# A planner that counts ScalarE's function tables, fewer filling products, and a split burst, in a two-layer recurrent trunk

## The chip, the cores and the metric

The kernel runs on one core of one Trainium2 chip. The metric is device time in microseconds (us) for one launch, the median of several executions. PE is the matrix engine (TensorE), DVE is VectorE, ACT is ScalarE, POOL is GpSimd and SP is the engine that issues most DMAs.

## The reference

One step of a two-layer decoder trunk over 1024 prompt tokens and 32 sample tokens (8 sequences of 4), width 1024, in fp32. Layer 1 is an RG-LRU block, layer 2 an HGRN2 block.

```python
def _rmsnorm(x, gain):
    return x * lax.rsqrt(jnp.mean(x * x, axis=-1, keepdims=True) + EPS) * gain

def _lru_layer(...):                          # layer 1
    u = _rmsnorm(x) @ w_in                    # 1024 x 3072
    xb, gate = u[..., :W_LRU], u[..., W_LRU:]
    xc = causal_conv(xb)                      # 4 taps
    r, ig = sigmoid(xc @ w_r + b_r), sigmoid(xc @ w_i + b_i)   # 16 blocks of 96
    a = exp(-8 * softplus(-lam) * r)
    h = scan(a, sqrt(1 - a * a) * ig * xc)
    return x + (h * silu(gate)) @ w_out       # 1536 x 1024

def _hgrn_layer(...):                         # layer 2, 8 heads of 128
    q, f, v, gate = split(_rmsnorm(x) @ w_in) # 1024 x 4096
    g = lb + (1 - lb) * sigmoid(f); k = 1 - g
    o, S = chunked_linear_recurrence(silu(q), k, v, log(g))
    return x + (norm(o) * silu(gate)) @ w_out # then a final rmsnorm
```

## The kernel before, in words

All 1056 tokens lie along the free axis, in three chunks of 352 (in layer 2's second half in quarters of 264). Every fp32 weight and activation is split into a high and a low part, and `mm3` (lines 246 to 251) makes one product of 128 input rows as three matmuls, high by high, high by low, low by high. A product over 1024 input rows is eight such steps into one of the `mm` banks of PSUM; the next product into a bank waits until the earlier one has been read. In the `hg` banks lie all smaller products: the norms' sums and their spread over the partitions, the LRU gates, the attention of layer 2.

**The order is written by a planner.** Each operation is recorded in a `Flow` with its engine, a cost in us, what it reads and writes, and a priority. `plan` runs a list schedule over these costs, `back` turns it into due times, `run` repeats this eight times and `search` tries 3000 random changes of the due times in the first 60 us; then the operations are emitted, engine by engine, in the planned order. Products of the main chain (`main=True`) keep the order in which they were recorded; everything else is placed by the planner. The hardware follows that order on each engine, whatever the times turn out to be. Layer 1 with the first products of layer 2 is one `Flow`, the rest a second.

**The start.** The weights and the first chunk come in by DMA. ACT makes the high parts (L390 for weights, L872 for activations), DVE the low parts (L333, L878), ACT the squares (L442), DVE adds them (L445). The first chunk's six products (three of the gates, three of the convolution; their weights lie in `whi`, `X`, `yh` and `yl`) use activations that are not yet normalised. `norm` follows for each of the three chunks: PE sums the squares over the partitions (L286), ACT takes three square roots (L457), DVE inverts them (L459) and lays them on diagonals (L460, L463), and PE spreads them by a product with ones (L465). The first chunk's products are scaled by this when they are read (L539, L492), the other chunks' activations before they are used (L470, L333). Filling products of ones by ones (L740), `WARM` of them, have the lowest priority: the planner places one where PE would otherwise have nothing.

**Function tables.** ACT computes Sqrt from one table and Tanh, Exp and Silu from another; plain copies, squares and scalings need neither. Where the function needs the table that is not loaded, an ACT_TABLE_LOAD stands in the instruction stream. The planner before knows of none: it charges 0.8 us for a norm's first square root and 2.5 us for the LRU's long one (L598).

**Layer 2.** Each head's small products come in four bursts between the large products. `burst2` holds two levels of the attention of head h (`levels24`: 64 products of 32 by 32 in the `diag` helper, L1068, and one for the samples, L1102), the chunk states of head h-1 (`states`: 32 products of 32 by 128, L1221, and 8 for the samples, L1230) and one product that advances the sample states (`advance`, L1251). From head 1 on, `seven` makes two projections with seven products of quarter width instead of eight; a string such as `126b754b3` gives the order, with `b` for a burst and each digit for two halves of 264 columns. Five banks of PSUM serve the bursts in turn.

## Time and profile before

| | |
|---|---|
| runs | 1057.6, 1057.96 and 1056.6 us; median 1057.6 us |
| the profiled execution | 1057.09 us, with a span of 1055.3 us |
| busy | PE 98%, DVE 75%, ACT 56%, POOL 48% |
| granted PE clock | 0.997 |
| PE's records | 10244 matmuls and as many weight loads |

The span runs from the first instruction's start to the last one's end, and 1.8 us of the run lie around it. A matmul's shown duration includes its way through the array and overlaps the next one's; the cost of one is therefore read from the distance between two starts. An fp32 product that is not split leaves two records for each matmul, a split one leaves one. PE is busy nearly all the time, so the question for every part of the program is where PE does work that the result does not need, and where it stands still.

### The profile page before, as it was taken

The page shows a single profiled execution, that of the slowest core. Times are in us where ns is not written, and L with a number is a line of the kernel's source. Part 1 is how long each engine was busy: PE and PEld are TensorE (multiplying, and loading weights), DVE is VectorE, ACT ScalarE, POOL GpSimd, SP SyncE. Part 2 cuts the span into 40 slices and gives each one's busy share as a digit, 9 for nine tenths or more (in the row PEclk, how much of TensorE's full clock was granted, in tenths as well). Part 3 has the DMA queues.
Part 4 walks back from the last instruction along what each step waited for, and adds up shares of the span by engine and source line. Part 5 has one row for each costly group of instructions (what it writes and reads, how often), then busy time and mean ns, then how long its engine had stood idle before and what let it go on. Part 6 is the DMA issues. An engine that isn't in the chain of part 4 may idle for free.

```text
span 1055.3 us, 26461 instructions
## 1 busy us (share of the span) xinstructions
PE 1037.3 (98%) x10244; PEld 1006.9 (95%) x10244; DVE 795.6 (75%) x1600; ACT 594.2 (56%) x1350; POOL 503.7 (48%) x569
## 2 busy tenths in 40 slices
PE   9899999999999999999999999999999999999997
PEld 9799999999999999999999999999999998999986
DVE  6999867778778689435597998897879796985436
ACT  8769646865865776334454363636454454662324
POOL 0116344534535345634636656564646555552544
PEclk9999999999999999999999999999999999999998
DMA  8201112122771487526554142333324242576204
GB/s 288 79 9 56 44 54 72 47 63 66 222 219 57 118 265 223 162 90 211 176 157 157 58 135 98 110 105 100 126 74 142 84 142 84 168 244 200 86 1 165
DMA packets 92013, 130.72 MB, mean 124 GB/s; under 512 B 11632, under 2 KB 70000, under 8 KB 91888
## 3 DMA queue, kind: packets, MB, share of 16 engines
q1 hardware_dynamic: 89584, 126.28, 37.9%
q10 hardware_dynamic: 2304, 2.77, 0.7%
q8 instruction: 80, 1.31, 0.5%
q14 instruction: 45, 0.37, 0.1%
HBM read 85.93 MB, written 38.20 MB: 118 GB/s over the span
## 4 chain that ended last, share of the span: by engine, by line
PE 92%; DVE 3%; ACT 2%; DMA 1%; issue 1%; POOL 0%; SPq 0%; ACTq 0%; POOLq 0%; DVEq 0%
PE mm L249 26%; PE mm L250 25%; PE mm L251 25%; PE hg L1068 2%; PE hg L579 1%; PE hg L1276 1%; PE hg L1278 1%; PE hg L249 1%; PE hg L251 1%; PE hg L250 1%; PE mm L1221 1%; PE hg L1221 1%; PE hg L1320 1%; DMA sg<-in_xT_dram 1%; ACT L457 0%
## 5 line engine op out<-in xcount | busy, mean ns | idle before, releaser
L249 PE MATMUL mm<-xh,whi 128*128 128x352 f32 (+1 forms) x1127 | 351.6, 312 | 0.0
L251 PE MATMUL mm<-xh,wlo 128*128 128x352 f32 (+1 forms) x1127 | 348.0, 309 | 0.0
L250 PE MATMUL mm<-xl,whi 128*128 128x352 f32 (+1 forms) x1127 | 347.9, 309 | 0.0
L333 POOL TENSOR_TENSOR wlo<-wraw,whi 128x256 fp32r<-128x256 f32 (+3 forms) x188 | 214.9, 1160 | 180.1 <-ACT whi L390 92.6
L250 PEld LDWEIGHTS mm<-xl,whi 128*128 128x128 f32 x1127 | 212.1, 188 | 1.5
L249 PEld LDWEIGHTS mm<-xh,whi 128*128 128x128 f32 x1127 | 211.9, 188 | 1.6
L251 PEld LDWEIGHTS mm<-xh,wlo 128*128 128x128 f32 x1127 | 212.3, 188 | 0.0
L511 DVE SCALAR_TENSOR_TENSOR k<-xb,prm_sb,k 128x352 f32<-128x352 f32 (+2 forms) x144 | 81.2, 588 | 24.7 <-ACT k L508 21.7
L249 PE MATMUL mm<-t,whi 128*128 128x264 f32 (+1 forms) x330 | 96.5, 292 | 0.0
L250 PE MATMUL mm<-t,whi 128*128 128x264 f32 (+1 forms) x330 | 94.4, 286 | 0.0
L251 PE MATMUL mm<-t,wlo 128*128 128x264 f32 (+1 forms) x330 | 94.4, 286 | 0.0
L1506 DVE TENSOR_TENSOR k<-mm,k 128x264 f32<-128x264 f32 x154 | 64.4, 424 | 30.1 <-PE mm L251 27.6
L594 POOL TENSOR_TENSOR k<-X 128x352 f32<-128x352 f32 x36 | 43.3, 1208 | 72.5 <-DVE R L595 66.1
L333 POOL TENSOR_TENSOR wlo<-R,whi 128x256 fp32r<-128x256 f32 x70 | 57.4, 841 | 36.9 <-ACT whi L1433 36.7
L390 ACT CAST whi<-wraw 128x512 fp32r<-128x512 f32 (+2 forms) x79 | 44.2, 573 | 33.2 <-PE mm L250 23.4
L249 PEld LDWEIGHTS mm<-t,whi 128*128 128x128 f32 x330 | 62.1, 188 | 0.6
L251 PEld LDWEIGHTS mm<-t,wlo 128*128 128x128 f32 x330 | 62.2, 188 | 0.0
L250 PEld LDWEIGHTS mm<-t,whi 128*128 128x128 f32 x330 | 62.1, 188 | 0.0
L1433 ACT CAST whi<-wraw 128x512 fp32r<-128x512 f32 x56 | 34.6, 617 | 46.9 <-DVE wraw L1443 17.5
L249 PE MATMUL mm<-yh,whi 128*128 128x352 f32 x153 | 52.2, 341 | 0.0
L250 PE MATMUL mm<-yl,whi 128*128 128x352 f32 x153 | 49.4, 323 | 0.0
L251 PE MATMUL mm<-yh,wlo 128*128 128x352 f32 x153 | 49.4, 323 | 0.0
(464 smaller groups left out, 2527.3 us busy)
## 6 DMA issues: line engine op xcount, KB each, us to landing
wraw<-in_w_dram SPq DMA_DIRECT2D x88, 256.0 KB, 2.9
wraw<-in_wo_dram SPq DMA_DIRECT2D x34, 192.0 KB, 2.6
R<-in_w_dram SPq DMA_DIRECT2D x17, 256.0 KB, 2.8
si<-in_s_in_dram SPq DMA_DIRECT2D x8, 512.0 KB, 4.5
vt<-sg SPq DMA_DIRECT2D x8, 512.0 KB, 3.2
kt<-kt SPq DMA_DIRECT2D x8, 512.0 KB, 2.7
sg<-vt SPq DMA_DIRECT2D x32, 128.0 KB, 3.0
kt<-kt SPq DMA_DIRECT2D x32, 128.0 KB, 3.7
```

The lines of the kernel that those rows point to most:

```text
L249: T.matmul(out, wh, xh, start=first, stop=False)
L250: T.matmul(out, wh, xl, start=False, stop=False)
L251: T.matmul(out, wl, xh, start=False, stop=last)
L333: emit = lambda: e.tensor_tensor(b, x, a.bitcast(F32), op=ALU.subtract)
L390: act(m, lambda hi=hi, raw=raw, m=m: S.copy(hi[:, :m], raw[:, :m]), rk, (hk,), prio)
L511: dve(u, lambda src=src, dst=dst, sh=sh, k=k: V.scalar_tensor_tensor(dst, sh(src, k), pc("cw", 12 * k + m), dst, op0=ALU.mult, op1=ALU.add ...
L579: fl.add("PE", 0.62, lambda ps=ps, i=i, c=c: T.matmul(ps[:96, :CH], gs[:, i, :], ST[:96, chunk(c)], start=True, stop=True), (("gs",), *((" ...
L594: pool(CH, lambda x=x, a=a, b=b: G.tensor_tensor(x, a.bitcast(F32), b.bitcast(F32), op=ALU.add), (ak, bk), (xk,), 3)
L1068: T.matmul(ps[32 * j:32 * j + 32, n * w:n * w + w], B[:, o:o + 32], q(slice(o, o + 32)), start=True, stop=True, tile_position=(0, 32 * j))
L1221: T.matmul(ps[w, n * 128:(n + 1) * 128], kt[:, 4 * i + n, a], vt[:, 4 * i + n], start=True, stop=True, tile_position=(0, 32 * a))
L1433: act(512, lambda: S.copy(hi, raw), (rk,), (hk,), 2)
L1506: dve(QT, lambda: V.tensor_tensor(o[0], z[0], u[0], op=ALU.add), (z[1], u[1]), (o[1],), 0)
```

## The change

Four things change, the first three in the planner's knowledge.

1. The planner learns the two tables. It finds out from an ACT operation's code which table it needs, starts with the second one loaded (`first=2`), charges 1.29 us whenever the other table is needed, and adds the same 1.29 us to such an operation's due time when ACT has to choose. The two hand-set charges for Sqrt fall to those of a plain operation. Some PE costs in layer 2 are changed by up to 0.15 us.
2. `WARM` is 36 instead of 48.
3. In layer 2, `burst2` first runs `levels24` alone. `states` and `advance` become a rest that `seven` runs after the first half of the next large product. They get a bank `t` of their own, so that a head takes 16 turns of the five banks instead of 15. The copy of `ab` moves to a later burst, since `states` of the earlier head must still read it.
4. Where `burst2` is called elsewhere, the rest runs at once.

```diff
-WARM = 48
+WARM = 36
...
+    SETS = {"Sqrt": 1, "Tanh": 2, "Exp": 2, "Silu": 2}
+    SWAP = 1.29
...
+        self.sets.append(next((self.SETS[o] for o in emit.__code__.co_names if o in self.SETS), 0) if eng == "ACT" else 0)
...
+        loaded = self.first
...
-            i = min((j for j in q if ready[j] <= t0), key=lambda j: (key[j], j))
+            if e == "ACT":
+                i = min((j for j in q if ready[j] <= t0), key=lambda j: (key[j] + (self.SWAP if self.sets[j] not in (0, loaded) else 0.0), j))
+            else:
+                i = min((j for j in q if ready[j] <= t0), key=lambda j: (key[j], j))
...
+            if self.sets[i] not in (0, loaded):
+                loaded = self.sets[i]
+                us += self.SWAP
...
-                    0.1 if i else 0.8)
+                    0.08)
...
-                act(3 * CH, lambda ta=ta: S.activation(ta, ta, AF.Sqrt, scale=0.25), tak, tak, 3, 2.5)
+                act(3 * CH, lambda ta=ta: S.activation(ta, ta, AF.Sqrt, scale=0.25), tak, tak, 3, 0.1)
...
         def burst2(h):
             s = next(hg)
-            run(together([*([levels24(h, *s)] if h < H else []), *([states(h - 1, *s), advance(h - 1, 0)] if h else [])]))
+            t = next(hg) if h < H else s
+            run(together([levels24(h, *s)] if h < H else []))
+            return (lambda: run(together([states(h - 1, *t), advance(h - 1, 0)]))) if h else None
...
-                    next(bursts)()
+                    rest = next(bursts)()
...
                     pe(1.475, emit, (*wk, *(k for o in ops for k in o[2])), (pk,))
+                    if rest:
+                        rest()
+                        rest = None
```

The changed file's lines stand 12 (start) to 21 (end) lower, so L740 is L752 there, L457 is L469, L465 is L477, L1221 is L1233.

**ACT, the first chunk's norm.** In the rows, `nr_132` and `nr_133` hold the roots of the first and the second chunk, `xo`, `R` and `xb` squares, `smalls` the prepared constants, `yh` weights. Before:

```order
L795 ACTIVATE smalls<-smalls 128x8
L457 ACT_TABLE_LOAD
L457 ACTIVATE nr_132<-hg,eps 128x1
L796 ACT_TABLE_LOAD
L796 ACTIVATE smalls<-smalls 128x8
L390 CAST yh_154<-ST 128x512
L457 ACT_TABLE_LOAD
L457 ACTIVATE nr_132<-hg,eps 128x1
L442 ACTIVATE xo_140<-R 128x352
L457 ACTIVATE nr_132<-hg,eps 96x1
```

Now, from the first norm to the end of the second:

```order
L469 ACT_TABLE_LOAD
L469 ACTIVATE nr_132<-hg,eps 128x1
...
L469 ACTIVATE nr_132<-hg,eps 96x1
...
L469 ACTIVATE nr_133<-hg,eps 128x1
L454 ACTIVATE xo_141<-R 128x352
L469 ACTIVATE nr_133<-hg,eps 128x1
L402 CAST yh_156<-wraw 128x512
L469 ACTIVATE nr_133<-hg,eps 96x1
L454 ACTIVATE xo_139<-R 128x352
L454 ACTIVATE xo_140<-R 128x352
L897 COPY R<-hg 128x352
L454 ACTIVATE xo_141<-R 128x352
L780 ACT_TABLE_LOAD
```

The two Exp of the constants (L795, L796) went behind both norms, which now share one load. Over the whole program 38 loads become 34.

**PE, around the spread of the second chunk's norm.** Before, 13 of the 48 filling products and the spread (L465) stand between the fifth and the sixth product of the first chunk (`yh_155` and `yh_156`):

```order
L249 MATMUL mm<-xh,yh_155 128x352
L250 MATMUL mm<-xl,yh_155 128x352
L251 MATMUL mm<-xh,yl_158 128x352
L740 MATMUL hg<-ones 128x128 x13
L465 MATMUL hg<-k,ones 128x352
L249 MATMUL mm<-xh,yh_156 128x352
L250 MATMUL mm<-xl,yh_156 128x352
L251 MATMUL mm<-xh,yl_159 128x352
```

Now the spread (L477) stands in the middle of the fifth, without a filling product:

```order
L261 MATMUL mm<-xh,yh_155 128x352
L262 MATMUL mm<-xl,yh_155 128x352
L263 MATMUL mm<-xh,yl_158 128x352
L477 MATMUL hg<-k,ones 128x352
L261 MATMUL mm<-xh,yh_155 128x352
```

In all of PE's order the filling products stood as 25, 9, 1 and 13, and now stand as 26, 4, 1, 1, 2 and 2; the last two lie just ahead of the second chunk's sums.

**PE, the second burst of head 1.** Before, levels, states and advance follow each other:

```order
L251 MATMUL mm<-xh,wlo 128x264
L1068 MATMUL hg<-R,a 32x32 x32
L1102 MATMUL hg<-R,a 32x32
L1068 MATMUL hg<-R,sg 32x32 x32
L1221 MATMUL hg<-sg,kt 32x128 x16
L1221 MATMUL mm<-sg,kt 32x128 x16
L1230 MATMUL hg<-si,ab 32x128 x8
L1251 MATMUL hg<-vb,kst 128x512
L249 MATMUL mm<-xh,whi 128x264
```

Now twelve matmuls of a large product, of which the first three are shown, stand between the levels and the states:

```order
L1080 MATMUL hg<-R,a 32x32 x32
L1114 MATMUL hg<-R,a 32x32
L1080 MATMUL hg<-R,sg 32x32 x32
L261 MATMUL mm<-xh,whi 128x264
L262 MATMUL mm<-xl,whi 128x264
L263 MATMUL mm<-xh,wlo 128x264
...
L1233 MATMUL mm<-sg,kt 32x128 x16
L1233 MATMUL hg<-sg,kt 32x128 x16
L1242 MATMUL hg<-si,ab 32x128 x8
L1263 MATMUL hg<-vb,kst 128x512
```

The same stands at the second burst of heads 1 to 7. Otherwise PE's order in layer 2 is the same as before.

32 lines of the change are left out of this document (19 added, 13 removed).

## The prediction, made before the change was run

> **What bounds the kernel now.** I read the page first: busy shares and the chain that ended last, by engine.
>
> ```profile
> PE 1037.3 (98%) x10244; PEld 1006.9 (95%) x10244; DVE 795.6 (75%) x1600; ACT 594.2 (56%) x1350; POOL 503.7 (48%) x569
> ...
> PE 92%; DVE 3%; ACT 2%; DMA 1%; issue 1%; POOL 0%; SPq 0%; ACTq 0%; POOLq 0%; DVEq 0%
> ```
>
> PE is the bound, so an edit is worth what it takes out of PE's time: waits, or work that the result doesn't need. Busy time by stretch says where that lies; the columns are the stretch, its length, then PE, PE's weight loads, DVE, ACT and POOL, the clock and the DMA share.
>
> ```profile
> 20.00:30.00 10.00, 8.70 (x54) 8.01 (x52) 6.37 (x21) 9.50 (x20) 0.00 (x0) 1.00 0.56 194
> 30.00:40.00 10.00, 8.41 (x58) 7.82 (x57) 7.63 (x16) 9.13 (x17) 2.42 (x4) 1.00 0.49 149
> 40.00:50.00 10.00, 8.03 (x44) 6.36 (x43) 9.80 (x22) 6.19 (x14) 0.91 (x3) 1.00 0.17 53
> ...
> 50.00:500.00 450.00, 449.93 (x2754) 443.39 (x2755) 332.82 (x598) 286.41 (x567) 200.37 (x221) 1.00 0.38 115
> ```
>
> From 50 to 500 us PE has nothing to give. Between 20 and 50 it has, and part of what counts as busy there is filling. The timeline of PE at the start (start, shown duration, instruction, and in brackets idle time with its releaser) shows both:
>
> ```profile
> 1.03 7.93 PE L740 MATMUL hg<-ones 128*128 128x128 f32 x50 [1.03 <-DVE nr L352]
> 8.72 0.41 PE L249 MATMUL mm<-xh,whi 128*128 128x352 f32 x1
> ...
> 9.77 2.17 PE L740 MATMUL hg<-ones 128*128 128x128 f32 x18
> 11.70 0.41 PE L249 MATMUL mm<-xh,whi 128*128 128x352 f32 x1
> ...
> 18.76 0.67 PE L286 MATMUL hg<-ones,xb 128*128 128x1 f32 x6
> 19.29 0.41 PE L249 MATMUL mm<-xh,X 128*128 128x352 f32 x1
> ...
> 23.22 0.33 PE L249 MATMUL mm<-xh,yh 128*128 128x352 f32 x1
> ...
> 25.68 0.78 PE L286 MATMUL hg<-ones,R 128*128 128x1 f32 x6 [0.84 <-DVE R L445]
> 26.91 0.86 PE L465 MATMUL hg<-k,ones 128*128 128x352 f32 x2 [0.46 <-DVE k L463]
> ...
> 31.29 0.43 PE L249 MATMUL mm<-xh,yh 128*128 128x352 f32 x1 [1.11 <-DVE sg L539]
> ...
> 35.26 3.06 PE L740 MATMUL hg<-ones 128*128 128x128 f32 x26
> 38.80 0.86 PE L465 MATMUL hg<-k,ones 128*128 128x352 f32 x2 [0.48 <-DVE k L463]
> ...
> 43.25 0.43 PE L249 MATMUL hg<-X,gh 128*128 128x352 f32 x1 [1.05 <-ACT X L516]
> ...
> 46.51 0.32 PE L249 MATMUL mm<-xh,X 128*128 128x352 f32 x1
> ```
>
> The reader is to see that the filling products are not free. Those at 9.77 and 35.26 stand in PE's order ahead of work that counts, 1.93 us (9.77 to 11.70) and 3.54 us (35.26 to 38.80, with the 0.48 behind them). The waits between 24 and 45 all end with DVE or ACT on the way to a norm or to a convolution. The row at 46.51 is the first product of the second chunk; I use it as a milestone.
>
> Why DVE is late there, ACT and DVE show:
>
> ```profile
> 19.54 1.28 ACT L457 ACT_TABLE_LOAD   x1
> 20.83 0.26 ACT L457 ACTIVATE nr<-hg,eps 128x1 f32<-128x1 f32 x1
> 21.10 1.28 ACT L796 ACT_TABLE_LOAD   x1
> ...
> 23.13 1.28 ACT L457 ACT_TABLE_LOAD   x1
> ...
> 30.93 1.28 ACT L540 ACT_TABLE_LOAD   x1
> ...
> 33.11 1.28 ACT L457 ACT_TABLE_LOAD   x1
> ```
>
> ```profile
> 22.63 0.17 DVE L785 TENSOR_TENSOR smalls<-smalls 128x8 f32<-128x8 f32 x1 [2.03 <-ACT smalls L796]
> ...
> 35.21 0.69 DVE L333 TENSOR_TENSOR yl<-wraw,yh 128x512 fp32r<-128x512 f32 x1 [1.50 <-ACT yh L390]
> ```
>
> Between the first and the last of these loads ACT changes tables five times, 6.4 us, inside two norms of three tiny roots each. In that time it makes no squares and no high parts, so DVE stands (2.03 and 1.50 us), and PE behind it.
>
> **The change at the start.** Removed from PE: 12 filling products. Moved: both Exp of the constants and the Tanh of the first gate go behind the second norm, so that ACT takes one load ahead of both norms and one behind. Four loads of 1.28 us leave the program, 5.1 us of ACT; all of it lies in this stretch.
>
> I sum PE up to the milestone. One step of three matmuls costs 0.491 us (24 matmuls of `X` from 19.29 to 23.22), a filling product 0.214 us (nine in 1.93), in the first stretch 0.308 us (25 from 1.03 to 8.72), a norm's sums 0.53 (18.76 to 19.29), its spread 0.86. Now the first stretch has 26 fillings: it ends at 1.03 + 26 x 0.308 = 9.03. Then come 48 steps, 23.6; ten fillings, 2.1; two sums, 1.1; two spreads, 1.7. Together 37.5. Before, the milestone stands at 46.51, and PE had done the third chunk's sums (0.53) and one gate product of three matmuls (0.49) by then that now come later: 45.5. The start is worth **8.0 us if no new wait comes**.
>
> Whether one comes I follow along the new order. The last high part of the first chunk is made near 10.6 on ACT, since two squares now stand behind it (before, 11.0), and nothing on DVE delays its low part to 12.7; the eighth step starts near 14. The first sums end at 19.0; ACT's roots with their one load end by about 22.5, and the spread is due at 25.7. The second sums are due at 23.8, some 2 us after DVE's last addition. The copy of the first spread follows it, and DVE frees the first bank near 28, when PE wants it at 28.5. The second spread is due at 30.5, its diagonal ready near 28.5. Then eight scalings and eight low parts on DVE, in the order of the steps, run from 31.5 to about 39.5, and the steps use them from 37.5 on, at 0.49 us each: the last one has about 1.5 us to spare. These margins are an estimate from durations such as those above. The least of them is half a microsecond, so a wait or two may come: bounds 0 and 4.5 us (as much as DVE's idle time above plus its nearest wait, 1.05), and I take 0.4, near the lower end, since the order puts the late operands first. **Start: 7.6 us.**
>
> From there to 500 us only the places of small products move. PE has 0.07 us idle there now; I take no gain and no loss, and keep -1 to +2 us for it. Between the chunks DVE could become late; that is a rival below.
>
> **The change in layer 2.** No product is added; one half of a large product is moved ahead of `states`. Behind it stand the second half, then two large products before the next burst, which needs what DVE makes of `states`. In the trace of PE, the second bursts of heads 1, 2, 4 and 6 hold waits; head 3, quoted between, has none.
>
> ```profile
> 591.94 0.85 PE L1221 MATMUL hg<-sg,kt 128*32 128x128 f32 x22
> 594.09 0.49 PE L1221 MATMUL hg<-sg,kt 128*32 128x128 f32 x9 [1.29 <-issue]
> ...
> 650.23 0.63 PE L1230 MATMUL hg<-si,ab 128*32 128x128 f32 x12
> 651.28 0.41 PE L1230 MATMUL hg<-si,ab 128*32 128x128 f32 x4 [0.42 <-issue]
> ...
> 702.75 0.73 PE L1068 MATMUL hg<-R,a 128*32 128x32 f32 x62
> ...
> 704.13 1.08 PE L1221 MATMUL hg<-sg,kt 128*32 128x128 f32 x32
> 705.00 1.08 PE L1221 MATMUL mm<-sg,kt 128*32 128x128 f32 x32
> ...
> 759.77 0.86 PE L1221 MATMUL mm<-sg,kt 128*32 128x128 f32 x22
> 761.65 0.52 PE L1221 MATMUL mm<-sg,kt 128*32 128x128 f32 x9 [1.02 <-issue]
> ...
> 869.89 1.08 PE L1221 MATMUL hg<-sg,kt 128*32 128x128 f32 x32
> 872.66 1.08 PE L1221 MATMUL mm<-sg,kt 128*32 128x128 f32 x32 [1.69 <-DVE a L1242]
> ```
>
> Undisturbed, 32 records take 0.87 us (704.13 to 705.00). So the four places lose 1.55 (2.15 for 22 records), 0.61 (1.05 for 12, at the same pace with a tenth more), 1.28 and 1.90: 5.3 us. Three have no releaser, and the fourth names a DVE instruction that reads this burst's result and can't release it. What they share is their place. I counted PE's instructions from the program's start, two for a split matmul or a transpose, four for an fp32 product: the waits stand at 8385, 10178, 13506 and 16834, that is 1793, 3328 and 3328 apart, 7, 13 and 13 times 256 but for one instruction. And the page has
>
> ```profile
> q8 instruction: 80, 1.31, 0.5%
> ```
>
> 80 packets for 2 x 10244 records: one for 256. **These are waits for the next block of instructions.** From passing one boundary inside the levels (estimated at 0.0105 us for a record: 702.75 to 704.13 for 132) to going on at the next, the four took 3.3, 3.4, 3.5 and 3.7 us.
>
> The filling products only change place, and their number shifts the boundaries; with the new order I find them, from the first instruction of the levels, at 96 and 352, 201 and 457, 52 and 308, 159 and 415, 10 and 266, 117 and 373, and 224 and 480 for heads 1 to 7. The levels now take 1.38 us for 264 instructions, the half product about 1.47 (twelve matmuls at three quarters of 0.164), the states 1.74 for the next 128. The second boundary comes 3.15, 4.3, 2.8, 3.6, 1.3, 3.3 and over 4 us after the first. Against 3.5 that leaves waits of 0.35, 0.7 and 0.2 in heads 1, 3 and 6. Head 5's pair begins at the first instructions of the levels, as head 3's did before at 8 and 264, and that one waited for nothing; I count zero. Left: 1.25 us, **gain 4.0 us**, bounds 0 (the waits only move) and 5.3.
>
> One more bank in each turn of five costs nothing I can find: every bank is taken again five takes later, and DVE's copy that frees the levels' bank (`attns`) now stands ahead of the two longer ones.
>
> **Sum.** 7.6 + 4.0 = 11.6 us, made against the profiled execution: 1057.09 - 11.6 = 1045.5. The median of the runs lies 0.5 above it: **1046.0 us**.
>
> **The rivals.** *DVE sets the pace.* DVE is busy 9.80 of the ten us from 40 on. If PE comes 8 us earlier and DVE can't, the start gains only what DVE's two waits on ACT give back, 3.5 us: 1057.6 - 3.5 - 4.0 = 1050.1. For it: those tenths; against it: much of that work is the LRU's, which nothing on PE wants for long. Chance 0.16.
>
> *The burst's waits stay.* If they come from banks or from data, or if the blocks merely fall elsewhere, layer 2 gives nothing: 1057.6 - 7.6 = 1050.0. For it: the trace names DVE for the longest; against it: the spacing of 256. The Trainium skill (Runtime: NRT & Kernel Launch, section Instruction fetch mechanics) says that the next block is fetched while the current one runs and that crossing a boundary is mostly hidden; by that rule this rival holds, and the four waits here speak against it for bursts of small products. Chance 0.13. Both rivals together: 1054.1, chance 0.03.
>
> *Slower.* The planner now adds 1.29 us to the due time of a square root when the other table is loaded, so ACT puts off the LRU's twelve long ones (L598) behind casts and Tanh. Each feeds a scan and an output product. The waits from this would lie between 60 and 470 us, where PE has none now; it decides from about 1 us of wait at each of the twelve (12 x 1.0 against 11.6). At 1.2 each: 1057.6 - 11.6 + 14.4 = 1060.4. Against it: the number of these loads stays, and the planner's length for them hardly changes (2.5 before, 1.29 for each switch now). Chance 0.05. *The order is no better on the chip than the old one*, about 1057.5: chance 0.03.
>
> **How the numbers follow.** The forecast has 0.60. The range, 1043.0 to 1051.5, reaches from both bounds on the good side (8.0 and 5.3, with 1 us between) across both single rivals. A measurement here can't tell less than about 0.2% from no change (the three runs spread over 0.13%). Faster by more than that: 0.60 + 0.16 + 0.13 + 0.03, less a little for waits I don't see, 0.90; within it 0.04; slower 0.06.
>
> **What would show it.** Start: the filling products at their six places, no wait above 0.5 us on PE between 13 and 40 us, two loads on ACT between 18 and 31 us, and the second chunk's first `X` step near 38 us (45.5 for no gain, 42 for the DVE rival). Layer 2: no waits named issue above 0.8 us in the second bursts, and those that remain in heads 1, 3 and 6. The forecast fails if PE waits for DVE between 40 and 120 us, or if PE is idle for more than 1 us between 50 and 500.

## The result, and the profile after the change

The changed kernel takes 1043.26 us (median of 4 runs, 1042.26 to 1043.57), the kernel before in the same comparison 1057.78 (4 runs, 1056.60 to 1058.51): ratio 0.9862, 95% interval 0.9845 to 0.9879, that is 14.5 us less. The forecast was 1046.0 us in a range of 1043.0 to 1051.5. The profiled execution took 1043.33 us with a span of 1041.5; before it was 1057.09 and 1055.3, so the two traces differ by 13.8 us, and this is what has to be found in them.

The busy shares and the chain that ended last, by engine, of the changed kernel:

```profile
PE 1033.0 (99%) x10220; PEld 1003.9 (96%) x10220; DVE 796.2 (76%) x1600; ACT 588.0 (56%) x1346; POOL 495.4 (48%) x569
...
PE 98%; DVE 1%; issue 0%; POOL 0%; POOLq 0%; ACT 0%
```

The chain was 92% PE before and is 98% now; the 3% of DVE, 2% of ACT and 1% of issue have almost gone. PE has 24 records less (12 filling products) and ACT 4 table loads less. Busy time by stretch (columns as in the prediction: stretch, length, PE, its weight loads, DVE, ACT, POOL, clock, DMA):

```profile
20.00:30.00 10.00, 10.00 (x65) 9.60 (x64) 9.27 (x23) 9.98 (x27) 0.59 (x1) 1.00 0.78 254
30.00:40.00 10.00, 10.00 (x62) 9.79 (x61) 10.00 (x21) 5.52 (x14) 2.86 (x3) 1.00 0.25 80
40.00:50.00 10.00, 10.00 (x67) 10.00 (x66) 10.00 (x29) 6.93 (x14) 2.29 (x5) 1.00 0.17 50
50.00:500.00 450.00, 450.00 (x2757) 443.33 (x2757) 333.46 (x605) 291.43 (x576) 206.80 (x227) 1.00 0.38 118
```

PE has no hole left between 20 and 500 us. DVE is now full from 30 to 50 us, where it was busy for 7.63 and 9.80 of ten before.

PE's timeline at the start, and ACT's table loads there:

```profile
1.03 7.46 PE L752 MATMUL hg<-ones 128*128 128x128 f32 x52 [1.03 <-DVE nr L364]
8.25 0.41 PE L261 MATMUL mm<-xh,whi 128*128 128x352 f32 x1
...
25.33 0.75 PE L477 MATMUL hg<-k,ones 128*128 128x352 f32 x2
...
29.96 0.75 PE L477 MATMUL hg<-k,ones 128*128 128x352 f32 x2
...
36.33 0.32 PE L261 MATMUL mm<-xh,X 128*128 128x352 f32 x1
```

```profile
18.54 1.28 ACT L469 ACT_TABLE_LOAD   x1
27.15 1.28 ACT L780 ACT_TABLE_LOAD   x1
45.11 1.28 ACT L469 ACT_TABLE_LOAD   x1
```

There are two loads between 18 and 31 us as forecast (before there were four, three of them between 19.5 and 24.5), no row between 9 and 40 us carries a wait, and the milestone, the second chunk's first `X` product, stands at 36.33 us; 38 was forecast, 46.51 was before.

The second bursts of heads 1, 3 and 6, the three in which a wait was expected to remain (the states, L1233):

```profile
582.03 1.08 PE L1233 MATMUL mm<-sg,kt 128*32 128x128 f32 x32
583.22 1.08 PE L1233 MATMUL hg<-sg,kt 128*32 128x128 f32 x32
...
637.34 1.95 PE L1233 MATMUL hg<-sg,kt 128*32 128x128 f32 x64
...
692.33 2.34 PE L1233 MATMUL hg<-sg,kt 128*32 128x128 f32 x62
...
858.81 1.25 PE L1233 MATMUL hg<-sg,kt 128*32 128x128 f32 x30
```

The row at 637.34 (head 2) is an undisturbed one: 64 records shown as 1.95. Head 3 shows 2.34 for 62, head 6 1.25 for 30, and in head 1 the second half of the states starts 1.19 us after the first, where an undisturbed head has 0.90. From the first matmul of the states to the next large product an undisturbed head takes 2.65 us; heads 1, 3 and 6 take 2.96, 3.15 and 2.96. So each of the three still loses 0.3 to 0.5 us.

**Where the 13.8 us are.** I cut both traces at four rows: the first product, the milestone, the first matmul of the levels of head 0 (543.90 before, 532.24 after) and that of head 7 (925.24 and 910.24).

| stretch | before | after | difference |
|---|---|---|---|
| to the first product | 8.72 | 8.25 | 0.47 |
| first product to milestone | 37.79 | 28.08 | 9.71 |
| milestone to the levels of head 0 | 497.39 | 495.91 | 1.48 |
| levels of head 0 to those of head 7 | 381.34 | 378.00 | 3.34 |
| levels of head 7 to the end | 130.06 | 131.26 | -1.20 |

At the milestone PE had done 1.02 us of work before that it does later now, as the prediction counted; so the start is worth 9.2 us up to there and 2.5 behind it, 11.7 together. Layer 2 gives 3.3, and the end takes back 1.2. Part of the start's figure is luck of this one execution: its first product came earlier than in any other trace with the same 26 filling products ahead of it (8.25 against 8.49 to 9.81).

### The profile page after: what moved, and what is told of

The parts are those of the page before. It is cut to its first block, busy times and chain, and to the rows that moved or that the text cites. A ratio compares the mean times of both kernels' runs of the same rounds, so it can differ in the third digit from the quotient of the medians.

```text
span 1041.5 us, 26438 instructions
## 1 busy us (share of the span) xinstructions
PE 1033.0 (99%) x10220; PEld 1003.9 (96%) x10220; DVE 796.2 (76%) x1600; ACT 588.0 (56%) x1346; POOL 495.4 (48%) x569
## 4 chain that ended last, share of the span: by engine, by line
PE 98%; DVE 1%; issue 0%; POOL 0%; POOLq 0%; ACT 0%
PE mm L261 27%; PE mm L263 27%; PE mm L262 27%; PE hg L1080 2%; PE hg L591 1%; PE hg L1233 1%; PE hg L261 1%; PE hg L263 1%; PE hg L262 1%; PE hg L1288 1%; PE hg L752 1%; PE hg L1290 1%; PE hg L1263 1%; PE hg L1332 1%; PE mm L1080 1%
## 5 line engine op out<-in xcount | busy, mean ns | idle before, releaser
L345 POOL TENSOR_TENSOR wlo<-wraw,whi 128x256 fp32r<-128x256 f32 (+3 forms) x188 | 205.2, 1108 | 198.9 <-ACT whi L402 79.6
L345 POOL TENSOR_TENSOR wlo<-R,whi 128x256 fp32r<-128x256 f32 x70 | 63.1, 921 | 33.7 <-ACT whi L1447 33.6
L606 POOL TENSOR_TENSOR k<-X 128x352 f32<-128x352 f32 x36 | 45.4, 1265 | 63.6 <-DVE R L607 34.0
L402 ACT CAST whi<-wraw 128x512 fp32r<-128x512 f32 (+2 forms) x79 | 43.7, 573 | 34.7 <-PE mm L262 20.3
```

What stands on the lines that cost most here:

```text
L345: emit = lambda: e.tensor_tensor(b, x, a.bitcast(F32), op=ALU.subtract)
L402: act(m, lambda hi=hi, raw=raw, m=m: S.copy(hi[:, :m], raw[:, :m]), rk, (hk,), prio)
L606: pool(CH, lambda x=x, a=a, b=b: G.tensor_tensor(x, a.bitcast(F32), b.bitcast(F32), op=ALU.add), (ak, bk), (xk,), 3)
```

## The experiments

My theory was that of the prediction: the start gains because ACT no longer changes tables inside the norms, and layer 2 because the four waits in the second bursts were waits for the next block of 256 instructions, which the half product now covers. Its rivals: the filling products alone carry the start; the waits of the bursts come from banks, from data or from DVE; the split does nothing and the waits only left with moved boundaries. Three things were open beside these: the 1.2 us at the end, what the filling products are for, and why the start was worth 4 us more than forecast.

All ratios are against the kernel before, run on the same chip. In the table each kernel's trace is cut at the rows named above; times in us.

| kernel | median | first product | to milestone | to head 0 | head 0 to 7 | to the end |
|---|---|---|---|---|---|---|
| before | 1057.4 to 1057.9 | 8.72 | 37.79 | 497.39 | 381.34 | 130.06 |
| the change | 1043.26 | 8.25 | 28.08 | 495.91 | 378.00 | 131.26 |
| tables alone | 1051.78 | 9.29 | 32.07 | 496.57 | 381.03 | 131.04 |
| 36 fillings alone | 1052.28 | 9.59 | 33.96 | 495.18 | 380.94 | 130.43 |
| both, no split | 1047.67 | 8.49 | 28.54 | 495.90 | 381.26 | 131.61 |
| split alone | 1054.61 | 9.06 | 38.11 | 497.48 | 378.33 | 130.72 |
| second planner without tables | 1043.38 | 9.76 | 27.91 | 495.91 | 377.03 | 130.79 |
| whole product in the burst | 1043.34 | 9.81 | 27.91 | 495.89 | 376.73 | 131.36 |
| 26 fillings, new order | 1046.58 | 9.77 | 28.52 | 495.89 | 377.97 | 132.55 |
| no filling | 1044.26 | 8.23 | 28.42 | 496.52 | 378.14 | 131.29 |
| the last two edits of the burst and the end | 1042.58 | 9.23 | 27.92 | 495.89 | 376.64 | 130.82 |
| the same, 18 fillings first | 1043.38 | 7.43 | 28.95 | 495.89 | 377.68 | 131.95 |
| the same, 18 fillings in all | 1042.22 | 6.54 | 29.75 | 495.90 | 377.22 | 131.29 |
| the same, one wait made longer | 1045.08 | 6.49 | 33.38 | 495.90 | 376.75 | 131.08 |

### The planner's tables alone

The change without the split burst and its cost figures, and with

```diff
-WARM = 36
+WARM = 48
```

> The kernel before with the planner's knowledge of ACT's tables alone: 48 fillings, second bursts in one piece. Its order has two table loads more within the two norms than the changed kernel's, and 22 fillings behind the first 26 instead of 10. Theory A (ACT's loads are what PE waited for at the start; the fillings only cost their own 0.214 us): the second chunk's first X product stands at 36.3 + 12 x 0.214 = 38.9 us, up to 41 with a wait left at the second norm; the bursts keep their 5.3 us of waits in heads 1, 2, 4 and 6, since each head's boundary lies where it lay; if it is this planning that lengthens the end, the end loses its 1.2 us here too. Time 1049.5 to 1052. Theory B (the twelve fillings carry the start, the loads were hidden): milestone above 43, time 1055 or more.

Measured: 1051.78 us, ratio 0.9944 (0.9932 to 0.9957), a gain of 5.9. The milestone stands at 41.36, 0.4 above theory A's 38.9 to 41, in an execution whose first product came 1.0 us later than in the change's trace. The time is A's, and theory B falls. A had allowed for a wait at the second norm; the two waits that are left stand behind the milestone instead:

```profile
41.36 0.61 PE L261 MATMUL mm<-xh,X 128*128 128x352 f32 x1
...
43.91 0.43 PE L262 MATMUL mm<-xl,X 128*128 128x352 f32 x1 [0.50 <-DVE xl L345]
...
45.34 0.43 PE L262 MATMUL mm<-xl,X 128*128 128x352 f32 x1 [0.67 <-DVE xl L345]
```

PE's waits between 24 and 50 us sum to 1.2 us; in the kernel before they sum to 4.7. But the number of loads isn't what tells the two apart. ACT loads a table six times between 18 and 46 us here (19.77, 26.48, 29.65, 32.61, 34.41, 37.60), seven times before and three times in the change. What differs is that the first norm's roots are no longer torn apart: one load at 19.77 and the next 6.7 us later, where the kernel before had 19.54, 21.10 and 23.13. That points to where the loads lie more than to how many there are; no run here separates the two. The waits in the bursts stayed where they were: head 1 keeps "[1.09 <-issue]", head 2 0.65, head 4 0.94, head 6 1.43.

### 36 filling products alone

The kernel before with

```diff
-WARM = 48
+WARM = 36
```

> The kernel before with 36 fillings instead of 48 and nothing else. The planner without knowledge of tables happens on an order with 34 table loads too (38 before), but with three roots of one norm still split by another table. Theory A (what counts at the start is the number of loads within the norms): milestone between 37 and 40 us, time 1050 to 1052 although the planner knows nothing of tables. Theory B (a planner without this knowledge leaves PE waiting, fewer fillings only turn into waits): milestone above 43, time 1055 to 1058. For the bursts: the block boundaries move by 48 instructions to 100, 206, 56, 162, 12, 118 and 224 of heads 1 to 7. If the waits are for instruction blocks, they stand in heads 1, 3, 4 and 6 with about 1.4, 1.6, 0.6 and 1.3 us; if they come from banks, data or DVE, they stay in heads 1, 2, 4 and 6 with 1.55, 0.61, 1.28 and 1.90.

Measured: 1052.28 us, ratio 0.9950 (0.9936 to 0.9964), a gain of 5.4. The planner, which here knows nothing of tables, happened on an order with three loads between 18 and 46 us, as few as the change has. Yet the milestone stands at 43.55. By theory A the time was to be 1050 to 1052 and the milestone 37 to 40, by theory B 1055 or more and above 43. The time lies 0.3 above A's and the milestone where B puts it, so neither holds as it stands: something else cost here. PE waits once, for the second norm, and then runs slowly:

```profile
37.05 1.13 PE L465 MATMUL hg<-k,ones 128*128 128x352 f32 x2 [1.94 <-DVE k L463]
...
43.84 0.49 PE L250 MATMUL mm<-xl,X 128*128 128x352 f32 x1
...
44.39 0.32 PE L249 MATMUL mm<-xh,X 128*128 128x352 f32 x1
```

```profile
36.00:38.00 2.00, 0.95 (x3) 0.60 (x4) 2.00 (x5) 0.48 (x1) 0.84 (x2) 0.88 0.17 46
38.00:40.00 2.00, 2.00 (x9) 2.00 (x8) 2.00 (x5) 0.81 (x3) 0.18 (x1) 0.50 0.93 300
...
44.00:46.00 2.00, 2.00 (x14) 2.00 (x12) 2.00 (x6) 0.68 (x3) 0.00 (x0) 0.92 0.00 0
```

The granted clock (the last column but two) is 0.50 from some 37.5 to 44.3 us, as the 0.88 and 0.92 of the outer stretches give it. In these 6.8 us the large matmuls stand 0.29 us apart instead of 0.16, so about 3 us are lost. I took this up in the last experiment.

For the bursts this run decides. The blocks' boundaries moved by 48 instructions, and the waits moved with them:

| waits in the second burst, us | head 1 | 2 | 3 | 4 | 5 | 6 |
|---|---|---|---|---|---|---|
| before | 1.68 | 0.82 | 0 | 1.43 | 0 | 1.90 |
| 36 fillings alone, expected for blocks | 1.4 | 0 | 1.6 | 0.6 | 0 | 1.3 |
| measured | 1.46 | 0 | 1.68 | 0.81 | 0 | 1.21 |
| both without split, expected for blocks | 1.4 | 0 | 1.55 | 0.61 | 0 | 1.28 |
| measured | 1.39 | 0 | 1.96 | 0.82 | 0 | 1.36 |

(Measured, and before: the time from the first matmul of the states to the next large product, less the 2.65 us of an undisturbed head.) PE's order in layer 2 is the same as in the kernel before. Head 3, which waited for nothing there, now waits:

```profile
697.96 0.92 PE L1221 MATMUL hg<-sg,kt 128*32 128x128 f32 x25
700.28 0.31 PE L1221 MATMUL hg<-sg,kt 128*32 128x128 f32 x4 [1.40 <-issue]
```

### The start without the split

The change without the split burst and its cost figures (36 fillings, tables known). Core of the difference to the changed kernel:

```diff
-            t = next(hg) if h < H else s
-            run(together([levels24(h, *s)] if h < H else []))
-            return (lambda: run(together([states(h - 1, *t), advance(h - 1, 0)]))) if h else None
+            run(together([*([levels24(h, *s)] if h < H else []), *([states(h - 1, *s), advance(h - 1, 0)] if h else [])]))
```

> The changed kernel without the split burst and its cost figures: 36 fillings and the planner's knowledge of tables. Theory A (the start is worth what the two traces show of it, about 10.7 us by 60 us): milestone 36.3 us, time 1057.8 - 10.7 - 0.6 (the bursts' waits are 4.7 instead of 5.3) + 0 to 1.2 (if the longer end belongs to this part) = 1046.5 to 1047.7. Theory B (the split also feeds the start or the stretch near 500 us): 1048.5 or more. For the bursts: boundaries at 96, 202, 52, 158, 8, 114 and 220 of heads 1 to 7, the offsets of before moved on by two heads. If the waits are for instruction blocks: about 1.4, 0, 1.55, 0.61, 0 and 1.28 us in heads 1 to 6; if banks, data or DVE: 1.55, 0.61, 0, 1.28, 0 and 1.90 as before.

Measured: 1047.67 us, ratio 0.9908 (0.9894 to 0.9921), at the upper edge of theory A's 1046.5 to 1047.7. The start gains 11.0 us by the levels of head 0, near the 6.0 and 5.2 of the two parts added up (which is chance in part, since the second has some 3 us of slow clock in it); the milestone is 37.03 (36.3 expected). The waits stand in heads 1, 3, 4 and 6, the places by blocks, and the longest is

```profile
692.10 0.86 PE L1233 MATMUL hg<-sg,kt 128*32 128x128 f32 x23
694.63 0.51 PE L1233 MATMUL hg<-sg,kt 128*32 128x128 f32 x9 [1.67 <-issue]
```

The end is 1.55 us longer than before, without any split.

### The split alone

The kernel before with the split burst and its cost figures (48 fillings, no knowledge of tables).

> The kernel before with the split burst and its cost figures alone: 48 fillings, no knowledge of tables, block boundaries within 2 instructions of where they lay before. Theory A (the half product gives the next block time to arrive): waits of about 0.4, 0, 0, 0.3, 0 and 0.3 to 0.6 us in heads 1 to 6 instead of 1.55, 0.61, 0, 1.28, 0 and 1.90; gain about 4.2 less 0.17 us in each of six heads, and less 1.2 if the longer end belongs to this part: time 1053.5 to 1055.8. Theory B (the waits only left with the moved boundaries, the split does nothing): four waits and 1057 to 1058.5.

Measured: 1054.61 us, ratio 0.9969 (0.9958 to 0.9980), a gain of 3.1, within theory A's 1053.5 to 1055.8; theory B falls. Between the levels of heads 0 and 7 it takes 378.33 us instead of 381.34. By the measure of the table the waits left in the states are 0.74 us in head 1 and 0.38 in head 6. Head 3, which waited for nothing before, now loses 0.45 ahead of its states, inside the half product; theory A had nothing there. The rows:

```profile
595.40 0.75 PE L1221 MATMUL mm<-sg,kt 128*32 128x128 f32 x20 [0.44 <-issue]
...
704.19 0.28 PE L250 MATMUL mm<-xl,whi 128*128 128x264 f32 x1 [0.29 <-issue]
```

### The end without tables

The changed kernel; the planner of layer 2 and the end does not know of tables:

```diff
-        fl = Flow(side=0.4, busy={e: ...})
+        fl = Flow(side=0.4, tables=False, busy={e: ...})
...
-                 if o in self.SETS), 0) if eng == "ACT" else 0)
+                 if o in self.SETS), 0) if eng == "ACT" and self.tables else 0)
```

> The changed kernel whose second planner (layer 2 and the end) doesn't know of tables; the first one still does. From 1010 us on, the changed kernel and both kernels that only plan by tables give back 0.8 to 1.1 us against the kernel before, the one with the split alone 0.3. Theory A (the rule, which lets ACT put single squares and roots of the last norms between each other, is what lengthens the end): the end gets 0.5 to 1.0 us shorter, time 1042.3 to 1042.8. Theory B (the end is longer because it is reached earlier, or by the split): time 1043.3, and the same order of squares and roots gives the same waits.

Measured: 1043.38 us (1042.74 to 1044.43), ratio 0.9866 (0.9852 to 0.9881): no gain in the median, as theory B has it. In the trace the end takes 130.79 us instead of 131.26, just under theory A's 0.5. With the rule, ACT puts a square between two pairs of roots, and the spread of that norm waits; in the changed kernel:

```profile
1014.00 1.28 ACT L1702 ACT_TABLE_LOAD   x1
1015.30 0.41 ACT L1702 ACTIVATE nr<-mm,eps 128x1 f32<-128x1 f32 x2
1015.63 0.44 ACT L1761 ACTIVATE a<-R 128x288 f32<-128x288 f32 x1
1015.98 0.40 ACT L1702 ACTIVATE nr<-mm,eps 128x1 f32<-128x1 f32 x2
...
1017.63 1.12 PE L1716 MATMUL hg<-sg,ones 128*128 128x512 f32 x2 [0.22 <-DVE sg L1706]
```

Without the rule the four roots stand together, and the spread (L1717 there) waits for nothing:

```profile
1015.66 0.72 ACT L1703 ACTIVATE nr<-mm,eps 128x1 f32<-128x1 f32 x4
...
1017.62 1.02 PE L1717 MATMUL hg<-sg,ones 128*128 128x512 f32 x2
```

In this one execution the gain is hidden by the first column of the table: the first product came at 9.76, in that of the change at 8.25, with the same 26 filling products before it. What the rule costs is shown for this wait alone: it stands in all six traces of kernels whose second planner knows of tables (0.20 to 0.22 us) and in none of the other eight. The rest of the 0.47 isn't: of the four kernels further down that have the same plan for the end, without the rule, three take 130.82, 131.08 and 131.29 us, and the fourth has a wait of its own there.

### The whole product in the burst

The changed kernel with both halves of the large product between levels and states:

```diff
-                    if rest:
+                    if rest and x:
```

> The changed kernel with the whole large product, both halves, between the levels and the states. Theory A (each block of 256 instructions needs some 3.5 us, and half a product more puts 1.5 us between the two boundaries): the waits left in the second bursts of heads 1, 3 and 6 (0.29, 0.36 and 0.27 us) go, no states part lasts longer than 1.8 us, gain 0.5 to 0.9: 1042.4 to 1042.8. Theory B (what is left there isn't for instructions, or the states are needed 1.5 us earlier than they now come): the states parts still last 2.0 us, or PE waits for DVE before the third bursts; 1043.3 or more.

Measured: 1043.34 us (1042.30 to 1043.51), ratio 0.9862 (0.9845 to 0.9878). The waits are gone, as by theory A, though its time of 1042.4 to 1042.8 is missed: the states take 1.77 us in each of the six heads, and the distance from one head's levels to the next is 54.98 or 54.99 us in all of them, where the change had 54.98 to 55.49. No wait for the later states appeared. The median shows nothing of the 1.3 us, again behind a first product at 9.81.

### Fewer filling products

The changed kernel with

```diff
-WARM = 36
+WARM = 26
```

> The changed kernel with 26 filling products, all ahead of the first product; the ten later ones are gone. Theory A (the ten stand where PE would wait for DVE's low parts anyway, since DVE is full from 8 to 18 us): milestone 35.8 to 36.4 us, waits of 1.5 to 2 us in sum on PE between 9 and 25 us, time 1043.0 to 1043.8; a single wait of 1.9 us would halve the clock for some 7 us, as in the kernel with fewer fillings alone, and cost 3 us more. Theory B (each filling costs its 0.214 us): milestone 34.2 us, time 1041.2. The block boundaries move by 40 instructions; 0 to 0.7 us of waits in the second bursts either way.

and with `WARM = 0`:

> The changed kernel without any filling product. The first product's operands are ready near 6.6 us, and the 26 fillings hold it back to 8.25. Theory A (the fillings bring the clock up and hold it): the first matmuls stand 0.29 us apart instead of 0.16 until the clock comes up, for 4 us or more of work, so that the milestone is at 36 to 40 us and the time 1043 to 1047. Theory B (the fillings only cost): first product at 6.6, milestone 32.6 to 34.5 us, time 1039.5 to 1041.5.

Measured: 26 fillings 1046.58 us, ratio 0.9898 (0.9883 to 0.9912); none 1044.26 us, ratio 0.9875 (0.9860 to 0.9889). The first answers neither theory. The planner found another order for it, with two waits at the first convolution (0.50 at 27.84 and 1.20 at 33.75), and its end is 1.3 us longer than the change's. The second speaks for theory A. Its first product came at 8.23 and not at 6.6, held back by ACT's high part, and the first matmuls do stand 0.29 us apart, for 5.6 us:

```profile
8.23 0.66 PE L261 MATMUL mm<-xh,whi 128*128 128x352 f32 x1 [8.23 <-ACT whi L402]
...
10.34 0.49 PE L261 MATMUL mm<-xh,whi 128*128 128x352 f32 x1
10.63 0.50 PE L262 MATMUL mm<-xl,whi 128*128 128x352 f32 x1
...
13.84 0.32 PE L261 MATMUL mm<-xh,whi 128*128 128x352 f32 x1
```

Still the milestone comes at 36.65, 0.3 us after the change's: what the slow clock costs (some 2.6 us) the ten later fillings that are gone (2.1) nearly pay for. All 36 filling products together are worth about 1 us by the medians; the intervals of the two ratios overlap.

### Both edits, and fewer fillings in the same order

The next three kernels keep the order that the planner made with 36 fillings and leave filling products out only when the instructions are written. First the two edits above together:

> The changed kernel with the two edits that gave nothing in the median apart: the second planner without tables, and the whole large product between levels and states. In their traces the end was 0.5 us shorter and the bursts kept no wait, but the first product came 1.5 us later than in the changed kernel's trace, at the same number of filling products. Theory A (the parts are real and small, and hidden by how early the clock rises in an execution): counted from the first product on, this kernel is 1.0 to 1.5 us shorter than the changed one; time 1042.0 to 1042.8. Theory B (no gain): counted from the first product as long as the changed one, time 1043.3.

Measured: 1042.58 us (1042.22 to 1043.19), ratio 0.9850 (0.9834 to 0.9866). Counted from the first product to the end of the span it takes 1031.3 us, the change 1033.3: 2.0 less, more than the 1.0 to 1.5 of theory A. The intervals of the two ratios overlap, so the median's 0.7 us isn't settled by these runs.

Then without the first 8 fillings:

```diff
+        def fill(i):
+            if i >= 8:
+                T.matmul(warm[:, :128], ones, ones, start=True, stop=True)
```

> The kernel before this one with the first 8 of the 26 filling products left out of the program and everything else in the same order. Theory A (the first fillings delay the first product: its operands are there at 6.6 us, and 26 fillings last until 8.25 or 9.8, by when the clock rises): first product at 6.6 to 6.9, DVE's low parts then set the pace of the first chunk, whose last one ends at 12.35; the milestone comes 0.7 us earlier than in an execution with an early clock and 2 us earlier than in one with a late clock; time 1040.5 to 1041.7. Theory B (the fillings are needed to bring the clock up, or DVE is the bound to 36 us): the time stays at that of the kernel before this one, 1042 to 1043.3.

and without the first 8 and the ten later ones (`if 8 <= i < 26`):

> As the last one, and the ten later fillings are left out too, with the same order otherwise (the kernel with 26 fillings had a new order from the planner). Theory A (the ten stand where PE would wait for DVE, and hide nothing else): PE waits instead, 2.1 us in sum between 9 and 25 us, none of the waits above 1 us, clock at 1.00; the time is that of the last kernel within 0.4 us. Theory B (they cost): milestone 2.1 us earlier, time 1038.5 to 1039.6.

Measured: 1043.38 us, ratio 0.9857 (0.9841 to 0.9874), and 1042.22 us (1041.43 to 1042.56), ratio 0.9845 (0.9829 to 0.9861). The three milestones are the answer: 36.33 in the change (first product at 8.25), 36.38 (7.43) and 36.29 (6.54). The start no longer follows the first product. What PE saves it waits for DVE, at the latest at the first convolution:

```profile
27.98 0.43 PE L262 MATMUL mm<-xh,yh 128*128 128x352 f32 x1 [0.62 <-DVE sg L552]
```

```profile
8.59 0.43 PE L263 MATMUL mm<-xl,whi 128*128 128x352 f32 x1 [0.30 <-DVE xl L895]
...
27.90 0.43 PE L262 MATMUL mm<-xh,yh 128*128 128x352 f32 x1 [1.13 <-DVE sg L552]
```

The upper row is of the kernel with 18 fillings first, the two lower ones of that with 18 in all. So in this order DVE bounds the start at 36.3 us: theory B of the 18 fillings in its second form, with a time 0.1 above its 1043.3. In the last kernel the waits sum to 2.1 us, as expected, but more than half of that is the one wait at 27.90. Theory A of the ten later ones holds for the start, not for the time, which was to agree within 0.4 us and differs by 1.2. That the kernel with the ten is slower comes from two places in layer 2: 0.7 us between the levels of heads 0 and 1, with a wait of 0.83 us for DVE at 578.37 (0.3 of it is won back at the next head), and 0.7 us behind the levels of head 7, with a wait of 0.58 us for DVE in its third burst. I have no cause for either. The last kernel has the lowest median of all; against the change (0.9862, 0.9845 to 0.9879) its interval overlaps.

### One wait made longer

The last kernel, with the DVE instruction for which PE waits 1.13 us at 27.90 made four times:

```diff
-dve(CH, lambda: V.tensor_tensor(sg, ps[:, :CH], by[0], op=ALU.mult), ...)
+dve(CH, lambda n=slow.pop() if slow else 0: [V.tensor_tensor(sg, ps[:, :CH], by[0], op=ALU.mult) for _ in range(1 + n)], ...)
```

> The last kernel (18 filling products first, none later) with one DVE instruction of the first convolution's gate made four times instead of once (the product into sg that frees the bank for which PE waits 1.13 us at 27.9 us). Each more takes some 0.44 us, so that wait becomes about 2.4 us. Theory A (a single wait of about 2 us on PE halves its clock for some 7 us, as the kernel with fewer fillings alone seemed to show behind its wait of 1.94 us): granted clock 0.5 from about 29 us on for 6 to 7 us, matmuls 0.29 us apart instead of 0.16, some 3 us lost beside the 1.3: milestone 39.5 to 41 us, time 1045.5 to 1047. Theory B (the clock fell there for another reason): clock 1.00 throughout, milestone 37.6, time 1043.3 to 1043.8.

Measured: 1045.08 us (1043.91 to 1045.45), ratio 0.9871 (0.9855 to 0.9888). The wait became 2.90 us, and the clock fell:

```profile
29.91 0.40 PE L262 MATMUL mm<-xh,yh 128*128 128x352 f32 x1 [2.90 <-DVE sg L553]
...
31.49 0.49 PE L262 MATMUL mm<-xh,yh 128*128 128x352 f32 x1
```

```profile
31.00:32.00 1.00, 1.00 (x6) 1.00 (x5) 1.00 (x3) 0.84 (x2) 0.65 (x2) 0.66 0.00 0
32.00:33.00 1.00, 1.00 (x4) 0.75 (x4) 1.00 (x2) 0.70 (x2) 1.00 (x1) 0.50 0.19 33
...
34.00:35.00 1.00, 1.00 (x6) 1.00 (x5) 1.00 (x3) 0.60 (x3) 0.37 (x1) 0.63 0.54 127
```

Theory A holds in kind: clock at half from 31.3 to some 34.7 us, milestone at 39.87 (39.5 to 41 expected, 37.6 without a fall of the clock). Its length was wrong: 3.4 us, half of the 6.8 in the kernel with 36 fillings alone, and 1.8 us lost (39.87 less 36.29 and the 1.77 by which the wait grew) instead of 3.

## Why the prediction was right, and where its sizes were off

**The mechanisms stood.** The forecast summed 7.6 us at the start and 4.0 in layer 2 to 1046.0; the change gave 11.7 and 3.3, less 1.2 at the end. The time fell into the range by little, and with luck: the start's 11.7 lie beyond even its upper bounds (8.0 and 2 behind the milestone), and without the 1.2 us at the end, which no term had, the median would lie near 1042, below the range.

**The start was sized too small, at four of its terms.** The filling products: 26 x 0.308 was to end at 9.03; the first product stands at 8.25. But 0.308 was one execution's figure, a mean over slow products ahead of the rise of the clock and fast ones behind it. The same 26 products end in seven other traces between 8.49 and 9.81, so this term varies by 1.6 us, and that it came out low here is luck. The spreads were put at 0.86 each; in the new order they show 0.75. The 0.4 us for new waits were not needed: no row from 9 to 40 us has one. And "from there to 500 us only the places of small products move" was the term that failed: 2.5 us came from there. The kernel before waited at 47.49, 49.14 and 50.07 (0.18, 0.14 and 0.18 in brackets, some 1.2 us in all behind the milestone by the distances of its rows), and 0.7 us more at a spread near 504 us; none of these is left, and the other 0.6 us I can't place. The prediction took the stretch from 50 us on as proof that nothing lies behind the milestone, though 3.5 us lie between the two, and it ended at 500, just ahead of the other wait.

**What carries the start** was told too simply. The prediction put it down to four loads less. The two parts gain 6.0 and 5.2 us apart and 11.0 together, by the levels of head 0. Tables alone still have six loads up to 46 us and gain; fewer fillings alone have three and lose about 3 us again to the clock. Together they leave no wait, and the clock stays up.

**DVE as the pace maker** had a chance of 0.16 with the milestone at 42. It didn't come true: PE is full in every stretch. But it was near. With fewer fillings ahead of the first product PE does wait for DVE, and the milestone stays at 36.3. In this order the start has come to DVE's limit.

**The bursts.** That the four waits of the kernel before are for blocks of 256 instructions is shown by the two kernels whose blocks lie elsewhere: in both the waits moved to the heads that the count gives. Five of the eight differ from the expected length by 0.1 us or less; head 4 is 0.2 longer in both, and one is 1.96 instead of 1.55. The rival of banks and data falls. One place the count doesn't explain: where a block's 256 instructions are the levels themselves (head 3 before, from 8 to 264), they are done in 1.3 us, and PE waited for nothing; with the split the same place costs 0.45 us. What is left of the waits was forecast as 1.25 us in heads 1, 3 and 6 (0.35, 0.7, 0.2). Against the undisturbed distance of 54.98 the heads lose 0.32, 0.51 and 0.28 there and 0.15 in others, 1.26 in all. So that term was right; the time lost before was a little more than the 5.3 counted (1.68, 0.82, 1.43 and 1.90 sum to 5.8, and 381.34 less 46.62 and six times 54.81 is 5.9). What was missing is the price of the split. An undisturbed head takes 54.81 us in the kernel before and 54.98 in the change, since PE passes once more between small and large products, and each passage costs about 0.1 us (0.22 and 0.21 us from start to start instead of 0.12): seven heads, 1.2 us. It is the step "no product is added" that failed. A product cut in two costs its seam.

**Where a boundary shows.** Beside large products the crossing of a boundary is hidden here, with 450.00 of 450.00 us busy from 50 to 500 in the change. In the bursts of the kernel before, where 256 instructions are done in less than about 3.5 us, PE waited 0.8 to 1.9 us at four of them. The Trainium skill (Runtime: NRT & Kernel Launch, section Instruction fetch mechanics) says that crossing a block's boundary is mostly hidden; the traces agree for the large products and not for these bursts.

**The end.** The forecast had nothing there. The rule by which a square root is put off was feared for the LRU's twelve long roots (the rival on the slower side); they cost nothing that the trace shows. It struck the four tiny roots of the last norms instead, where a wait of 0.22 us comes and goes with it. The other 1.0 us stays open. The split alone has an end 0.66 us longer than before, but the kernel with both other parts and no split has 1.55, and the kernel with 36 fillings alone, which has neither the split nor the rule, 0.37: the end's length follows no single part of the change.

**A version that is better than both** is likely but not shown: the change with the whole product in the burst, the second planner without tables and 18 fillings, 1042.22 us against 1043.26, in different comparisons and with ratios whose intervals overlap.

## What to carry to other kernels

A block of instructions has its price in time, not in work: here a stretch of PE that uses up 256 instructions in less than about 3.5 us waited for the rest, with the one kind of exception told above, and one whole large product between two groups of small ones removed the wait for the price of a seam of 0.2 us. Before small products are moved, count the instructions from the program's start: in two kernels the count told all eight waits by head, five of them to 0.1 us. And whoever sums a start from one trace should first see how the same instructions lie in another execution: the filling products alone moved it by 1.6 us.

## What the runs showed of the hardware that I had not expected

**The clock needs from 2.9 to 6.2 us to come up, by chance.** The filling products start at 1.03 us in each trace that has them. In the trace of the change their records stand 0.213 us apart up to 3.97 us and 0.112 us apart behind it. In that of the kernel whose second planner has no tables, with the same instructions up to there, the step comes only at 7.14. The first two rows are of the change, the others of that kernel:

```profile
3.00:4.00 1.00, 1.00 (x7) 1.00 (x7) 0.00 (x0) 0.89 (x1) 0.00 (x0) 1.00 1.00 352
4.00:5.00 1.00, 1.00 (x11) 1.00 (x11) 0.00 (x0) 0.38 (x1) 0.00 (x0) 1.00 1.06 352
```

```profile
3.00:4.00 1.00, 1.00 (x7) 1.00 (x7) 0.00 (x0) 0.89 (x1) 0.00 (x0) 1.00 0.96 330
...
6.00:7.00 1.00, 1.00 (x7) 1.00 (x7) 0.71 (x3) 1.00 (x4) 0.00 (x0) 1.00 1.04 289
7.00:8.00 1.00, 1.00 (x10) 1.00 (x10) 1.00 (x2) 1.00 (x3) 0.00 (x0) 1.00 0.94 270
```

There are 7 records in a microsecond ahead of the rise and 10 or 11 behind it. In the thirteen traces with filling products the rises lie between 3.97 and 7.26 us, 3.3 us apart. This is the 1.6 us between first products of 8.25 and 9.81; the clock's column shows 1.00 in either case, only the spacing of the records tells. The Trainium skill (TensorE: Matmul & The Clock Gate, Part 1) gives a free-running window of 3.4 us and says that the number of slow matmuls varies with its phase; the traces agree, with 3.3.

**A wait of 2 us can cost as much again.** Behind PE's waits of 1.94 and 2.90 us the clock was at half for 6.8 and 3.4 us, the longer fall behind the shorter wait. Behind waits of 1.11 and 1.20 us it stayed up, and behind the bursts' waits of 1.67 and 1.69 us too. The same page of the Trainium skill (Why this matters for your kernels) asks for no gap above some 3 us; here 1.94 us were enough once. Each wait is one execution. What decides between 1.69 and 1.94 us the runs don't show; the phase of that window could, and so could the kind of work around the wait.

**The end of a trace varies by half a microsecond** between kernels with the same order there (130.82, 131.08 and 131.29 for three that share the plan of the end), so an edit worth less than that can't be told from one trace.
